# Recurrence inputs as twelve paired seven-product sums, with outputs taken partly from the PSUM banks

## The chip, the core and the metric

The kernel runs on one core of one Trainium2 chip. Its metric is device time in microseconds, from one launch to the end of its last output. It runs one layer for one sequence of 512 tokens with 1024 channels, in float32.

## What is computed

The layer is a feed-forward block, two token mixers side by side, and a second feed-forward block, each with a normalization in front and behind and a residual. Cut to what matters here:

```
h = h + 0.5 * norm(swiglu(norm(h)))                      # FFN 1, d_ff 2816
u = norm(h);  q, k, v, xr, yr, gl = split(u @ w_in)      # one wide product
attn_d = attention(q, k, v) @ w_attn_branch              # 12 heads, three dilations
xc  = causal_conv4(xr);  ga, gx = sigmoid(xc @ w_a), sigmoid(xc @ w_x)   # per head
rec = scan(a(ga), b(ga, gx, xc)) * gelu(yr);  rec_d = rec @ w_rec_branch
g0, g1 = sigmoid(gl)                                     # a gate for each branch
h = h + norm((g0 * attn_d + g1 * rec_d) @ w_out)
h = h + 0.5 * norm(swiglu(norm(h)))                      # FFN 2
```

The change concerns the columns of `w_in` that give `xr`, `yr` and the second half of `gl`: 8 + 8 + 8 column blocks of 128, each a product of a 1024 x 128 weight with the 1024 x 512 activation `u`.

## The kernel before, in words

**Numbers in two halves.** A float32 operand is split into a high part (rounded to float32r by ScalarE, L261) and a low part (VectorE subtracts, L262). A product then takes three matmuls for each block of 128 contraction rows: high x high, high x low, low x high (`mm3`, L275 to L278). `split` is one ScalarE copy and one VectorE subtract, for weights as for activations.

**Weights** come in one stream in the order of `stream_plan` (L65), in loads of 1 MB into the two buffers of tile `raw`, issued by SyncE (L207). `fetch` (L219) splits a block into tile `w8`, which has four buffers of 2 x 1024 columns (or `w4`, two of 2 x 512).

**Two kinds of product.** The plain one, `gemm` (L291), makes one block of 128 output columns with 8 x 3 matmuls of 512 columns. The other, `seven` (L594), makes a pair of output blocks, called `g` and `u`, at once: by a Strassen-like scheme with seven products p1 to p7 on halves of the channels and halves of the tokens, each 4 x 3 matmuls of 256 columns. It needs sums of the activation's quarters (made once, `forms_of`, L507) and, for each pair, sums of the weight's quarters, each split again (`w_forms`, L557, and `w_forms_in_place`, L576). A pair's weights so take three splits of 1024 columns, one of 512, and four additions of 512 on VectorE; a plain block takes one split of 1024. Before the change the FFNs use such products (in `prod`, L841, with their own code), as do the twelve pairs of q and k and the four pairs of the first gate half (L1220). The recurrence uses plain products.

**The order around the change.** After FFN 1 (to about 356 us) come the values, then for each of four heads the q and k pairs and attention, then the four gate pairs, then the product with `w_attn_branch` (eight plain products of 4 x 3 matmuls). Then the recurrence: `conv(0)`; for each head `branch`, `conv` of the next head, `gates_of`, `recur`, and the plain products of the second gate half by the table `GATE1` (L41). `conv` makes two blocks of `xr`, copies them from the bank into an order by phase (L1281), and applies four taps (L1283, L1285); `branch` makes two blocks of `yr` and copies them (L1297); `gates_of` takes 24 matmuls and four sigmoids (L1314); `recur` is a chain of ScalarE functions (L1325 to L1340), VectorE products (L1330 to L1343), a scan (L1344), and a split into `rec` (L1346). Last, the product with `w_rec_branch` (L1364), `w_out`, and FFN 2.

A scheduler orders the instructions of each engine from the written order and from priorities (`tc.high_priority`); each engine then runs its own list in that order, waiting on semaphores. Eight PSUM banks are shared: `acc_ps` (L264) hands out banks 0 to 4 in turn, `aux_ps` banks 5 to 7.

Of the kernel before, what the change touches and what calls it, by code (L numbers as in the profile page):

```python
# [40 lines left out]
GATE1 = ((), (0, 1), (2, 3), (4, 5, 6, 7))  # L41
# [7 lines left out]
def ffn_order(n):  # L49
# [4 lines left out]
    for f in range(n0, NF):  # L54
# [6 lines left out]
        order.append(("finish", f))  # L61
    return order


def stream_plan():  # L65
# [37 lines left out]
    for h in range(-1, NH):  # L103
        if h >= 0:
            for c in (2 * h, 2 * h + 1):
                plan.append((("in", 44 + c), 1024))
        if h + 1 < NH:
            for c in (2 * h + 2, 2 * h + 3):
                plan.append((("in", 36 + c), 1024))
        if h < 0:  # L110
            continue
        plan.append((("lru", h), 1024))
        for c in GATE1[h]:
            plan.append((("in", 60 + c), 1024))
# [32 lines left out]
def hybrid_layer(ctx: ExitStack, tc: tile.TileContext, xT: bass.AP, xN: bass.AP, wst: bass.AP,  # L147
# [11 lines left out]
    turns = {"acc": 0, "aux": 0}  # L159
# [104 lines left out]
    def acc_ps():  # L264
        turns["acc"] += 1
        return banks[(turns["acc"] - 1) % 5]
# [150 lines left out]
    class Boundary:  # L417
# [3 lines left out]
        def __init__(self, f, grow, his, los, kept):  # L421
            self.f, self.grow, self.his, self.los, self.kept = f, grow, his, los, kept
            self.u = {}
# [13 lines left out]
        def turn(self, b):  # L437
            for i, u in enumerate(self.u.pop(b)):
# [4 lines left out]
                hi, lo = (t[:, :, b * P:(b + 1) * P] for t in (self.his[i], self.los[i]))  # L443
# [63 lines left out]
    def forms_of(x, his, los, pool, copied):  # L507
# [8 lines left out]
        def slot():  # L516
            return tx_slot(pool, 1 if copied else 2).rearrange("p s k t -> p s (k t)").rearrange(
                "p s (b c) -> p s b c", b=2)
# [3 lines left out]
        for name, i, j in (("p1", 0, 0), ("p2", 1, 0), ("p3", 1, 1)):  # L522
            t[name] = tuple(z[i][:, :, HALVES[j]] for z in (his, los))
# [20 lines left out]
        def middle():  # L544
            form("p6", slot(), d[2])
# [48 lines left out]
    def seven(t, w, z, g, u, seen=lambda ap: ap):  # L594


        b, y = acc_ps()[:, :HB], acc_ps()[:, :HB]
# [17 lines left out]
        def sum_of(dst, ps, c):  # L615
            with tc.high_priority(offset=EVAC):
                DVE.tensor_add(dst, seen(ps), seen(c))
# [895 lines left out]
```

## Time and profile before

| | before |
|---|---|
| median of 3 runs | 1247.98 us (1246.37 to 1248.45) |
| the profiled execution's own time | 1246.12 us |
| its span, first to last instruction | 1244.4 us |
| PE busy in the span | 1221.5 us, 98% |
| VectorE (DVE) busy | 958.9 us, 77% |
| ScalarE (ACT) busy | 730.1 us, 59% |
| granted TensorE clock | 0.997 |

In the profile, PE is TensorE, PEld its weight loads, DVE is VectorE, ACT ScalarE, POOL GpSimd and SP SyncE. A row of a timeline gives the start in us, the duration, engine, line, operation, output and inputs, and in brackets how long the engine sat idle ahead of it and what ended that. Matmuls are pipelined, so their durations overlap; the time from one start to the next tells what each takes of the stream.

### The profile page before, as it was taken

What the parts mean: (1) busy time and instruction counts of PE and PEld (TensorE: products, weight loads), DVE (VectorE), ACT (ScalarE), POOL (GpSimd) and SP (SyncE); (2) the same over time, 40 slices, a digit from 0 to 9 for tenths busy, and PEclk for the clock granted to TensorE, in tenths of its full rate; (3) what the DMA queues carried; (4) which work ended last, traced back from release to release, by engine and by line L of the source; (5) the groups of instructions that cost most, each with busy time, mean ns of one, the idle gap of its engine ahead of it and who ended that gap; (6) DMA issues with size and microseconds to landing.
All of it is one profiled execution on the core that took longest, in us unless ns stands there. A gap on an engine that the chain in (4) does not pass through costs nothing.

```text
span 1244.4 us, 19101 instructions
## 1 busy us (share of the span) xinstructions
PE 1221.5 (98%) x7616; PEld 1100.5 (88%) x7616; DVE 958.9 (77%) x1510; ACT 730.1 (59%) x1215; POOL 75.6 (6%) x123
## 2 busy tenths in 40 slices
PE   9979999999999999999999999999999999999997
PEld 8878999999877899999988787888899999999996
DVE  7997798988577487898665878655788887979865
ACT  7556665664455455665545988733566565656442
POOL 0001101010102000000000000000110110101000
PEclk9999999999999999999999999999999999999999
DMA  6245646464724132222242222323462555555441
GB/s 242 102 124 148 170 122 170 135 166 123 239 114 161 68 111 78 97 81 81 91 169 102 102 102 68 104 100 143 145 220 87 151 160 150 160 141 158 114 153 67
DMA packets 35449, 162.35 MB, mean 130 GB/s; under 512 B 3872, under 2 KB 7072, under 8 KB 23328
## 3 DMA queue, kind: packets, MB, share of 16 engines
q1 hardware_dynamic: 17712, 106.08, 24.1%
q0 software_dynamic: 17648, 55.06, 16.8%
q8 instruction: 59, 0.97, 0.3%
q14 instruction: 30, 0.25, 0.1%
HBM read 150.64 MB, written 6.29 MB: 126 GB/s over the span
## 4 chain that ended last, share of the span: by engine, by line
PE 78%; DVE 10%; ACT 7%; DMA 2%; issue 2%; SPq 0%; DVEq 0%; ACTq 0%
PE bank L853 9%; PE bank L854 9%; PE bank L855 9%; PE bank L276 5%; PE bank L277 5%; PE bank L278 5%; PE bank L605 4%; PE bank L606 4%; PE bank L607 4%; PE bank L769 4%; PE bank L770 4%; PE bank L771 4%; DVE w L262 2%; DMA raw<-in_w 2%; ACT w L261 1%
## 5 line engine op out<-in xcount | busy, mean ns | idle before, releaser
L262 DVE TENSOR_TENSOR w<-raw,w 128x1024 fp32r<-128x1024 f32 (+1 forms) x275 | 297.6, 1092 | 91.5 <-ACT w L261 87.7
L261 ACT ACTIVATE w<-raw 128x1024 fp32r<-128x1024 f32 (+1 forms) x275 | 255.5, 950 | 121.9 <-PE bank L278 44.9
L853 PE MATMUL bank<-big,w 128*128 128x256 f32 x840 | 241.4, 287 | 7.1 <-DVE ub L866 3.0
L854 PE MATMUL bank<-big,w 128*128 128x256 f32 x840 | 238.1, 283 | 0.0
L855 PE MATMUL bank<-big,w 128*128 128x256 f32 x840 | 236.8, 283 | 0.0
L853 PEld LDWEIGHTS bank<-big,w 128*128 128x128 f32 x840 | 161.3, 192 | 12.5 <-DVE ub L866 5.4
L854 PEld LDWEIGHTS bank<-big,w 128*128 128x128 f32 x840 | 161.5, 192 | 1.5
L855 PEld LDWEIGHTS bank<-big,w 128*128 128x128 f32 x840 | 160.9, 192 | 0.0
L605 PE MATMUL bank<-big,w 128*128 128x256 f32 x320 | 91.9, 287 | 0.0
L606 PE MATMUL bank<-big,w 128*128 128x256 f32 x320 | 91.7, 287 | 0.0
L607 PE MATMUL bank<-big,w 128*128 128x256 f32 x320 | 90.8, 284 | 0.0
L769 PE MATMUL bank<-wd,act 128*128 128x512 f32 x224 | 87.8, 392 | 0.0
L770 PE MATMUL bank<-wd,act 128*128 128x512 f32 x224 | 87.7, 392 | 0.0
L771 PE MATMUL bank<-wd,act 128*128 128x512 f32 x224 | 87.2, 389 | 0.0
L276 PE MATMUL bank<-big,w 128*128 128x512 f32 x192 | 74.7, 389 | 0.0
L278 PE MATMUL bank<-big,w 128*128 128x512 f32 x192 | 74.7, 389 | 0.0
L277 PE MATMUL bank<-big,w 128*128 128x512 f32 x192 | 74.7, 389 | 0.0
L861 ACT ACTIVATE c<-bank 128x256 f32<-128x256 f32 x72 | 27.5, 382 | 62.4 <-PE bank L855 61.9
L605 PEld LDWEIGHTS bank<-big,w 128*128 128x128 f32 x320 | 61.2, 191 | 1.1
L606 PEld LDWEIGHTS bank<-big,w 128*128 128x128 f32 x320 | 61.3, 191 | 0.0
L607 PEld LDWEIGHTS bank<-big,w 128*128 128x128 f32 x320 | 61.3, 191 | 0.0
L262 DVE TENSOR_TENSOR wd<-npair,wd 128x1024 fp32r<-128x1024 f32 x24 | 29.4, 1223 | 39.4 <-ACT wd L261 39.4
(344 smaller groups left out, 2976.1 us busy)
## 6 DMA issues: line engine op xcount, KB each, us to landing
raw<-in_w SPq DMA_DIRECT2D x94, 1024.0 KB, 5.0
dr<-in_wdn POOLq DMA_DIRECT2D x40, 512.0 KB, 5.4
npair<-in_wdn POOLq DMA_DIRECT2D x32, 512.0 KB, 5.5
big<-act POOLq DMA_DIRECT2D x6, 512.0 KB, 3.5
h<-in_x SPq DMA_DIRECT2D x8, 256.0 KB, 5.2
h<-in_xn POOLq DMA_DIRECT2D x4, 512.0 KB, 5.2
kept_m<-h POOLq DMA_DIRECT2D x4, 512.0 KB, 2.9
h<-kept_m POOLq DMA_DIRECT2D x4, 512.0 KB, 4.3
```

The costliest lines, as they stand in the source:

```text
L261: ACT.activation(dh, src, AF.Copy)
L262: DVE.tensor_sub(dl, src, dh.bitcast(F32))
L276: PE.matmul(ps, wh, xh, start=first, stop=False)
L605: PE.matmul(ps, wh, xh, start=start and k == 0, stop=False, skip_group_check=True)
L606: PE.matmul(ps, wh, xl, start=False, stop=False, skip_group_check=True)
L607: PE.matmul(ps, wl, xh, start=False, stop=k == 3, skip_group_check=True)
L769: PE.matmul(ps, xh, wh, start=start and k == 0, stop=False, skip_group_check=True)
L770: PE.matmul(ps, xh, wl, start=False, stop=False, skip_group_check=True)
L771: i = PE.matmul(ps, xl, wh, start=False, stop=k == 1, skip_group_check=True)
L853: PE.matmul(ps, wh, xh, start=start and k == 0, stop=False, skip_group_check=True)
L854: PE.matmul(ps, wh, xl, start=False, stop=False, skip_group_check=True)
L855: i = PE.matmul(ps, wl, xh, start=False, stop=k == 3, skip_group_check=True)
```

## The change

The 24 plain products of the recurrence's stage become twelve calls of `seven`. The table `GATE1` now lists pairs, placed one behind head 1, one behind head 2, two behind head 3. `seven` itself is rewritten for all its users: the order is p1, p5, p6, p2, p7, p3, p4; two banks of four are taken in turn, and a fifth, bank 4, is held for the half that takes p1 + p2, with p1 copied into it by ScalarE (from the second pair on); two of the four outputs are read straight from a bank by ScalarE, the other two are VectorE additions of a bank and a copy. The activation's forms must outlive attention, so p6 gets a buffer of its own (`six`) and p4 one of the six large ones; the residual `h` is therefore reloaded behind the recurrence and not ahead of the product with `w_attn_branch`. The 25 small VectorE operations on `a_param` now write into `npair`, a tile that is free from the end of FFN 1.

```diff
-GATE1 = ((), (0, 1), (2, 3), (4, 5, 6, 7))
+GATE1 = ((), (0,), (1,), (2, 3))
+def rec_order():
+    def pair(c):
+        return ("pair", c, c + 1)
+    order = [pair(36)]
+    for h in range(NH):
+        order.append(pair(44 + 2 * h))
+        if h + 1 < NH:
+            order.append(pair(36 + 2 * h + 2))
+        order.append(("lru", h))
+        order += [pair(60 + 2 * g) for g in GATE1[h]]
+    return order
...
-        return banks[(turns["acc"] - 1) % 5]
+        return banks[(turns["acc"] - 1) % turns["of"]]
...
-            form("p6", slot(), d[2])
+            form("p6", slot() if copied else six, d[2])
...
-            form("p4", big([P, 2, 2, T]) if copied else slot(), d[2])
+            form("p4", big([P, 2, 2, T]), d[2])
...
-    def seven(t, w, z, g, u, seen=lambda ap: ap):
-        b, y = acc_ps()[:, :HB], acc_ps()[:, :HB]
+    def seven(t, w, y, fresh, g0, g1, u0, u1):
+        b, z, y = acc_ps()[:, :HB], acc_ps()[:, :HB], y[:, :HB]
...
         product("p1", b, True)
-        c1 = copy(b)
-        product("p2", y, True)
-        sum_of(g[0], y, c1)
+        if fresh:
+            c1 = copy(b)
+        else:
+            out(lambda: ACT.activation(y, b, AF.Copy))
+        product("p5", z, True)
+        c5 = copy(z)
         product("p6", b, False)
         c6 = copy(b)
-        product("p5", z, True)
-        c5 = copy(z)
+        product("p2", y, fresh)
...
+            out(g0, y)
         product("p7", b, False)
-        c7 = copy(b)
-        sum_of(u[1], c7, c5)
-        product("p4", y, True)
-        sum_of(u[0], y, c7)
+        out(u1, b, c5)
         product("p3", z, False)
-        sum_of(g[1], z, c6)
+        out(g1, z, c6)
+        product("p4", b, False)
+        out(u0, b)
...
-        new_h()
-        for b in range(4):
-            nc.gpsimd.dma_start(hb(b), kept_m[b])
...
         def s8(name):
-            return lpool.tile([P, 8], F32, name=name)
+            i = 8 * next(s8s)
+            return npair[:, 0, i:i + 8]
...
+        def take(ev):
+            i = events.index(ev)
+            if i + 1 < len(events):
+                request(events[i + 1])
+            return ready.pop(ev)
+        def run(key, *outs):
+            seven(t, take(key), banks[4], False, *outs)
         def conv(hd):
-            for c in (2 * hd, 2 * hd + 1):
-                ps = acc_ps()
-                gemm(ps, fetch(("in", 36 + c)), um)
...
+            run(("pair", 36 + 2 * hd, 37 + 2 * hd),
+                lambda ps: ACT.activation(g0, seen(ps), AF.Copy),
+                lambda ps, c: DVE.tensor_add(g1, seen(ps), seen(c)),
...
         lpool_cm.__exit__(None, None, None)
+        turns["of"] = 5
+        new_h()
+        for b in range(4):
+            nc.gpsimd.dma_start(hb(b), kept_m[b])
```

`request` calls `w_forms_in_place` for a pair, so while one pair is multiplied the forms of the next are made. `branch` and the gate loop are rewritten in the same way as `conv`; the second gate half's outputs go through `gate_pair`, whose straight halves ScalarE's sigmoid reads from the bank, and whose other halves VectorE adds first.

**How rows move on VectorE, in the recurrence.** These rows of before stand in VectorE's list between the recurrence of head 1 and the taps of head 3's `xr`. A subtract into `w8` (L262) is one plain block's low half; L1285 is a tap, L1297 the copy of a `yr` block, L1345 the last product of `recur`:

```order
L1297 COPY ge_6953<-bank0_73 128x512
L262 TENSOR_TENSOR rec_6336<-ge_6688,rec_6336 128x512
L1345 TENSOR_TENSOR ge_6719<-th_6831,ge_6719 128x512
L262 TENSOR_TENSOR w8_7022<-raw_6984,w8_7022 128x1024
L262 TENSOR_TENSOR w8_7060<-raw_7058,w8_7060 128x1024
L262 TENSOR_TENSOR rec_6336<-ge_6719,rec_6336 128x512
L1297 COPY ge_6982<-bank1_74 128x512
L262 TENSOR_TENSOR w8_7131<-raw_7058,w8_7131 128x1024
L262 TENSOR_TENSOR w8_7161<-raw_7159,w8_7161 128x1024
L1285 SCALAR_TENSOR_TENSOR sig_6337<-xr_7013,first_83,sig_6337 128x512 x3
```

Of the change, the rows around the taps of head 1's `xr`. Line numbers are those of the changed kernel: L267 is the subtract of a split, L1359 a tap, L589 to L593 the four additions of a pair's weight quarters (`raw_6696` holds the pair of `yr` for head 1, `raw_6784` the pair of `xr` for head 2):

```order
L267 TENSOR_TENSOR w4_6701<-raw_6696,w4_6701 128x512
L1359 SCALAR_TENSOR_TENSOR sig_6307<-xr_6582,first_83,sig_6307 128x512
L589 TENSOR_TENSOR raw_6696<-raw_6696 128x512
L1359 SCALAR_TENSOR_TENSOR sig_6307<-xr_6584,first_83,sig_6307 128x512
L590 TENSOR_TENSOR raw_6696<-raw_6696 128x512
L267 TENSOR_TENSOR w4_6789<-raw_6784,w4_6789 128x512
L592 TENSOR_TENSOR raw_6696<-raw_6696 128x512
L589 TENSOR_TENSOR raw_6784<-raw_6784 128x512
L267 TENSOR_TENSOR w8_6700<-raw_6696,w8_6700 128x1024
L593 TENSOR_TENSOR raw_6696<-raw_6696 128x512
L590 TENSOR_TENSOR raw_6784<-raw_6784 128x512
L267 TENSOR_TENSOR rec_6306<-sig_6307,rec_6306 128x512
```

Where before one subtract of 1024 columns stood for each block, there is now a run of additions and subtracts for each pair, and the taps stand between them.

**How rows move on VectorE, at the end of FFN 1.** Before, between the second product's last additions into `facc` and the last output column's sums (`u`, L866, is the sum that must have read its bank before p4 may go on in it), there stood:

```order
L786 TENSOR_TENSOR facc<-facc,bank_76 128x512
L262 TENSOR_TENSOR act<-u,act 128x512
L786 TENSOR_TENSOR facc<-facc,bank_77 128x512
L262 TENSOR_TENSOR wd_98<-raw,wd_98 128x1024
L262 TENSOR_TENSOR w_3103<-raw,w_3103 128x1024
L866 TENSOR_TENSOR u<-bank_74,c 128x256
```

In the change all the small operations on `a_param` stand ahead of the last two of these (L878 is the same sum as L866); here are the last of them and what follows:

```order
L1316 TENSOR_TENSOR npair<-npair 128x8
L1318 SCALAR_TENSOR_TENSOR npair<-npair 128x8
L1319 TENSOR_SCALAR npair<-npair 128x8
L1320 TENSOR_SCALAR npair<-npair 128x8
L267 TENSOR_TENSOR w_3103<-raw,w_3103 128x1024
L878 TENSOR_TENSOR u<-bank_74,c 128x256
```

Before, they stood behind the last gate pair, some 300 us later. On ScalarE their one Exp moves with them, with a load of its function table, to just ahead of the copy of p1 for FFN 1's last output column.

More of the change, by code (lines that the diff above doesn't have):

```diff
@@ L102, in stream_plan @@
         plan.append((("attn", m), 512))
[L103 to L114, printed above, removed]
+    for ev in rec_order():
+        plan.append((ev, 1024 if ev[0] == "lru" else 2048))
     for m in range(KC):
@@ L1081, in pair_of, with pair @@
             return forms.pop(key)
+        def pair(key, *outs):
+            seven(t, pair_of(key), banks[4], first_pair.pop() if first_pair else False, *outs)
         def qk(hd):
@@ L1289, in branch @@
         def branch(hd):
-            gel = []
-            for c in (2 * hd, 2 * hd + 1):
-                ps = acc_ps()
-                gemm(ps, fetch(("in", 44 + c)), um)
-                ge = lpool.tile([P, T], F32, name="ge", tag="ge", bufs=4)
-                with tc.high_priority(offset=EVAC):
-                    DVE.tensor_copy(ge, ps)
-                gel.append(ge)
+            gel = [lpool.tile([P, T], F32, name="ge", tag="ge", bufs=4) for _ in range(2)]
+            (g0, g1), (u0, u1) = ([x[:, h] for h in HALVES] for x in gel)
+            run(("pair", 44 + 2 * hd, 45 + 2 * hd),
+                lambda ps: ACT.activation(g0, ps, AF.Copy),
+                lambda ps, c: DVE.tensor_add(g1, ps, c),
+                lambda ps: ACT.activation(u0, ps, AF.Copy, scale=-1.0),
+                lambda ps, c: DVE.scalar_tensor_tensor(u1, ps, -1.0, c, op0=ALU.mult, op1=ALU.subtract))
             return gel
         def gates_of(hd):
-            wh, wl = fetch(("lru", hd))
+            wh, wl = take(("lru", hd))
             a_ = wh.rearrange("p (w i c) -> p w i c", w=2, i=2)
@@ L1354, in hybrid_layer @@
             recur(hd, gel, gas, gxs)
[L1355 to L1358 removed]
+            for g in GATE1[hd]:
+                gate_pair(("pair", 60 + 2 * g, 61 + 2 * g), sig, 2 * g, run)
         lpool_cm.__exit__(None, None, None)
+        turns["of"] = 5
+        new_h()
+        for b in range(4):
+            nc.gpsimd.dma_start(hb(b), kept_m[b])
         mg = act_big("mg")
```

113 lines of the change are left out of this document (74 added, 39 removed).

## The prediction, made before the changed kernel ran

> **What bounds the kernel now.** I read the page's first two parts, then the windows of the recurrence's stage, then rows of its timelines.
>
> ```profile
> PE 1221.5 (98%) x7616; PEld 1100.5 (88%) x7616; DVE 958.9 (77%) x1510; ACT 730.1 (59%) x1215; POOL 75.6 (6%) x123
> PE   9979999999999999999999999999999999999997
> DVE  7997798988577487898665878655788887979865
> ```
>
> TensorE is busy in nearly every slice, so for most of the span only matmuls taken away or added count. VectorE is the second engine. In slices 20 to 25 (622 to 809 us) it falls to 5 to 8 tenths: the attention branch's product and the recurrence.
>
> ```profile
> core 0: us, PE busy (x) PEld busy (x) DVE busy (x) ACT busy (x) POOL busy (x), PEclk, DMA share, GB/s
> 648.50:664.00 15.50, 15.50 (x70) 12.82 (x69) 9.25 (x12) 7.80 (x9) 0.00 (x0) 1.00 0.34 132
> 664.00:704.00 40.00, 39.24 (x173) 32.15 (x172) 26.31 (x38) 30.15 (x39) 0.00 (x0) 1.00 0.30 105
> 704.00:744.00 40.00, 38.44 (x170) 31.49 (x169) 33.33 (x43) 32.24 (x42) 0.00 (x0) 1.00 0.26 90
> 744.00:784.00 40.00, 39.02 (x171) 31.69 (x170) 28.70 (x36) 34.90 (x45) 0.00 (x0) 1.00 0.27 96
> 784.00:805.30 21.30, 21.30 (x95) 17.64 (x95) 17.43 (x22) 17.37 (x23) 0.00 (x0) 1.00 0.28 97
> sum 156.80, PE 153.50 PEld 125.79 DVE 115.01 ACT 122.46 POOL 0.00; mean PE 30.70 PEld 25.16 DVE 23.00 ACT 24.49 POOL 0.00
> ```
>
> This is the stage that the change rewrites, 156.8 us long. TensorE works 153.5 of it and waits some 3.3; VectorE has 115.0 and ScalarE 122.5 (columns 1, 3 and 4 of the busy times). So the stage is TensorE's, with 42 us of room on VectorE and 34 on ScalarE. What the change takes from TensorE it pays for out of that room.
>
> **What TensorE saves.** Starts of successive matmuls, first of a plain product, then of a seven-product pair, and the first matmul of the product with `w_rec_branch`:
>
> ```profile
> 648.30 0.39 PE L276 MATMUL bank<-big,w 128*128 128x512 f32 x1
> 648.53 0.39 PE L277 MATMUL bank<-big,w 128*128 128x512 f32 x1
> 604.72 0.28 PE L605 MATMUL bank<-big,w 128*128 128x256 f32 x1
> 604.84 0.28 PE L606 MATMUL bank<-big,w 128*128 128x256 f32 x1
> 805.14 0.39 PE L276 MATMUL bank<-rec,w 128*128 128x512 f32 x1
> ```
>
> A matmul of 512 columns takes 0.227 us of the stream, one of 256 takes 0.120: more than half. Two plain blocks are 48 x 0.227 = 10.9 us; a pair is 84 x 0.120 = 10.1 us. The scheme that saves an eighth of the arithmetic saves 0.8 us a pair, 12 x 0.8 = 9.6 us in all. TensorE's work in the stage becomes 12 x 10.1 + 96 x 0.227 (the gates) = 142.8 us. The Trainium skill ("TensorE: Matmul & The Clock Gate", section Back-to-back issue gap) speaks against even this: it gives about 81 ns for a sustained matmul of 128 columns and 131 for one of 512, so an estimate half-way between is some 98 ns for 256, and twelve pairs would cost 12 x (84 x 0.098 - 48 x 0.131) = 23 us more than the plain blocks, where the rows say 9.6 less. The rows have these very tiles and decide.
>
> **What VectorE pays.** Rows from the recurrence and from an FFN:
>
> ```profile
> 706.84 1.22 DVE L262 TENSOR_TENSOR w<-raw,w 128x1024 fp32r<-128x1024 f32 x1
> 707.98 1.29 DVE L262 TENSOR_TENSOR rec<-ge,rec 128x512 fp32r<-128x512 f32 x2
> 709.18 0.75 DVE L1285 SCALAR_TENSOR_TENSOR sig<-xr,first,sig 128x512 f32<-128x512 f32 x1
> 162.34 0.69 DVE L584 TENSOR_TENSOR raw<-raw 128x512 f32<-128x512 f32 x1
> 163.06 0.69 DVE L585 TENSOR_TENSOR raw<-raw 128x512 f32<-128x512 f32 x1
> 169.24 0.42 DVE L866 TENSOR_TENSOR ub<-bank,c 128x256 f32<-128x256 f32 x1
> 169.58 1.22 DVE L262 TENSOR_TENSOR w<-raw,w 128x1024 fp32r<-128x1024 f32 x1
> ```
>
> and the groups of the stage, each shape apart:
>
> ```profile
> L262 DVE TENSOR_TENSOR w<-raw,w 128x1024 fp32r<-128x1024 f32 x29 | 35.1, 1220 | 18.0 <-ACT w L261 18.0
> L261 ACT ACTIVATE w<-raw 128x1024 fp32r<-128x1024 f32 x29 | 30.5, 1058 | 8.3 <-DMA raw<-in_w 5.3 <-PE bank L278 2.5 <-ACT ge L1340 0.6
> L1281 ACT ACTIVATE xr<-bank 128x512 f32<-128x512 f32 x8 | 8.7, 1089 | 11.1 <-PE bank L278 11.1
> L1297 DVE COPY ge<-bank 128x512 f32<-128x512 f32 x8 | 5.5, 682 | 5.2 <-PE bank L278 5.2
> ```
>
> Start to start, a subtract of 1024 columns takes 1.14 us, one of 512 takes 0.60, an addition of 256 0.34; an addition of 512 columns takes 0.72 behind another one of its chain (162.34 to 163.06) and, if it stands between strangers, no less than the 0.60 of the subtract; I take 0.66. The forms of a pair cost 3 x 1.14 + 0.60 + 4 x 0.66 = 6.7 us of VectorE, two plain blocks 2.3. Of the 29 subtracts in the stage four are for the gates and two for the next product, so 23 belong to plain blocks. VectorE's sum is then: 115.0, less 23 x 1.14 = 26.2, less eight copies of `yr` at 0.60 = 4.8, plus 12 x 6.7 = 80, less 3 for the first pair's forms that are made beside the attention branch's product, plus 24 additions of 256 at 0.36 = 8.6. That is 169.6 us. ScalarE: 122.5, less 23 x 1.05 and 8.7 and some 5 for reads of whole banks, plus 12 x (3 x 1.05 + 0.63) = 45 and some 68 reads of 256 columns at 0.27, is about 148 us. Its pace for 256 columns:
>
> ```profile
> 601.22 0.37 ACT L612 ACTIVATE c<-bank 128x256 f32<-128x256 f32 x1
> 601.48 1.06 ACT L261 ACTIVATE w<-raw 128x1024 fp32r<-128x1024 f32 x1
> ```
>
> So **the bound changes hands**: 142.8 us for TensorE, 148 for ScalarE, 169.6 for VectorE. The order shown above confirms where this falls: the taps and the recurrence's products stand between the rows of the forms, and TensorE's p5 and p6 wait for those. What is not for pairs is 169.6 - 77 - 8.6 = 84 us, 21 a head. Behind head 1, with three pairs of 6.7 + 0.7 us, VectorE so owes 43 us; TensorE has 3 x 10.1 + 24 x 0.227 = 35.7.
>
> **How long the stage gets.** When VectorE is the bound it does not work all the time. The one stretch of before where it bounds, the start of FFN 1, tells how much is lost:
>
> ```profile
> 28.00:78.00 50.00, 46.58 (x242) 39.96 (x240) 47.94 (x65) 27.10 (x36) 2.60 (x4) 0.97 0.34 116
> ```
>
> It works 47.94 of 50 us, 96%. 169.6 / 0.96 = 176.9 us to the last split into `rec`. The first block of the next product needs that split only for its last eighth, 4.8 us after its start, so TensorE may begin at about 172. In the first 60 us VectorE and TensorE are nearly even and wait for each other in turn; I add 1.5, a choice. 173.6 against 156.8 is **+16.8 us**. Without any loss on VectorE it would be 169.6 - 4.8 = 164.8, or +8.0: the lower end.
>
> **The end of FFN 1.** The small operations on `a_param` cost nothing before, since they stood beside the attention branch's product. Now they stand ahead of a sum for which TensorE waits:
>
> ```profile
> 634.69 0.17 DVE L1260 TENSOR_SCALAR po<-po 128x8 f32<-128x8 f32 x1
> 634.89 0.17 DVE L1261 TENSOR_TENSOR po<-po,zz 128x8 f32<-128x8 f32 x1
> 626.35 1.28 ACT L1252 ACT_TABLE_LOAD   x1
> 314.72 1.22 DVE L262 TENSOR_TENSOR wd<-raw,wd 128x1024 fp32r<-128x1024 f32 x1 [1.50 <-ACT wd L261]
> 319.37 1.23 DVE L262 TENSOR_TENSOR w<-raw,w 128x1024 fp32r<-128x1024 f32 x1 [3.43 <-ACT w L261]
> 320.52 0.42 DVE L866 TENSOR_TENSOR u<-bank,c 128x256 f32<-128x256 f32 x1
> 320.99 0.39 PE L853 MATMUL bank<-big,w 128*128 128x256 f32 x1
> ```
>
> VectorE's split at 314.72 ends at 315.9; ScalarE's table load and Exp put off the next step to about 316.1. 26 operations at 0.20 end at 321.3; the split that stood at 319.37 ends at 322.5, the sum of 320.52 at 322.9. TensorE's p4 began at 320.99, right behind that sum, so it comes **1.8 us** late, and what follows is a full TensorE. At least 0 (if the scheduler's gaps fit better on the chip), at most 5.2, the whole row of operations.
>
> **Attention and the rest.** Its pairs keep their number of matmuls, and TensorE has no gap there:
>
> ```profile
> 480.00:520.00 40.00, 40.00 (x330) 39.35 (x329) 33.85 (x69) 23.13 (x54) 0.00 (x0) 1.00 0.24 86
> L853 PE MATMUL bank<-big,w 128*128 128x256 f32 x840 | 241.4, 287 | 7.1 <-DVE ub L866 3.0 <-DVE g L866 2.5 <-ACT c L861 0.9
> ```
>
> Fewer VectorE sums can therefore gain nothing. The new order makes p4 wait until u1 has read bank b, with p3's 1.4 us as cover, as the FFNs' products already do; those show 7.1 us of idle time in 30 pairs, 5.5 of it two single waits. The other 1.6 over 30 pairs is 0.05 a pair; the whole is 0.24. For 16 pairs that is 0.9 to 3.8 us; I take **1**. The later reload of `h` is four loads on POOL's queue:
>
> ```profile
> h<-kept_m POOLq DMA_DIRECT2D x4, 512.0 KB, 4.3
> ```
>
> The product with `w_rec_branch` (192 x 0.227 = 43.5 us) lies between them and their first use: nothing, and at the worst one landing of 4.3 us. SyncE's queue has two more loads for the same bytes, at 0.26 to 0.34 of the DMA engines' time (last but one column of the windows): nothing, unless a buffer `raw` comes free late, which is part of the ring below.
>
> **The sum.** 1246.1 + 16.8 + 1.8 + 1.0 = 1265.7 us for an execution like the profiled one. That one lies 1.9 under the median of the runs, so I give **1267**.
>
> **Rivals.** *TensorE stays the bound.* If the forms were always ready, the stage would give back 9.6 us: 1246.1 - 9.6 + 2.8 for the other two terms, 1241 with the offset. For it: the FFNs run the same forms with TensorE full. Against it: there VectorE has room, here 169.6 us do not fit into 143. It decides if VectorE needs less than 10.1 us a pair with all else, and it needs about 14. 6%. *The gain and the loss cancel*, because the subtracts and sums overlap better than start to start and ScalarE takes the strain: within some 8 us above before, 1248 to 1256. 10%. *The ring of buffers takes over.* The third `w8` of a pair takes the place of the one that p3 of the pair before has read. From the end of p3 the chain is ScalarE's copy (1.06), VectorE's subtract (1.22), p5, p2, the additions and the last split, p6, p7, p3: about 10.2 us even if both engines were free. Whatever of VectorE's other 7 us a pair falls into it adds in full: at worst 17 us a pair, 12 x 17 = 204 us less the overlap of the gates, some 195, +38: 1289. For it: VectorE runs its list in order, and taps stand inside the forms. Against it: the order puts two pairs' forms beside each other, so the chain has other work to hide in. 16%. The forecast itself, VectorE's sum with a few per cent of loss, has 68%.
>
> **Range and chances.** The forecast's own range is 1256 to 1278. To hold 8 in 10 I go from 1253, the upper part of the cancelling case, to 1284, most of the way to the ring. A measurement of this kernel can tell about 0.2%, 2.5 us, from no change. Faster: 6%, the first rival. Same: 4%, the lower part of the second. Slower: 90%.
>
> **What would show it.** In the profile after, the stage from the attention branch's product to the product with `w_rec_branch` should be about 173 us, with VectorE busy for 160 to 170 of it and TensorE for some 143, and TensorE's waits there should name VectorE's splits `w` (L267). At the end of FFN 1 there should be one wait of TensorE of 1 to 2 us for the sum `u`. I am wrong if VectorE is busy below 90% of the stage while TensorE waits (then it is the ring or ScalarE), if TensorE is full there (then the forms were cheaper than their rows), or if attention shows waits of more than 4 us.

## The result, and the profile after

The changed kernel takes 1263.71 us (median of 4 runs, 1262.35 to 1265.16) against 1247.17 us before (4 runs): a ratio of 1.0134, with a 95% interval of 1.0122 to 1.0147. It is 16.5 us slower. The prediction was 1267 with a range of 1253 to 1284. The profiled execution of the changed kernel took 1263.51 us, with a span of 1261.7 us.

From the page of the changed kernel, busy times and slices:

```profile
PE 1225.2 (97%) x8048; PEld 1120.9 (89%) x8048; DVE 1003.0 (79%) x1567; ACT 760.4 (60%) x1307; POOL 75.7 (6%) x123
PE   9979999999999999999999889899999999999997
DVE  7997798988776587788478999965688888979865
```

TensorE's row now has slices of 8 tenths in the recurrence, 22, 23 and 25 (from 694 us on), and VectorE's slices 20 to 25 show 7 to 9 in place of 5 to 8. The windows of the recurrence's stage, which begins at 650.17 us behind the attention branch's product and ends at 822.78 us with the first matmul of the product with `w_rec_branch`:

```profile
core 0: us, PE busy (x) PEld busy (x) DVE busy (x) ACT busy (x) POOL busy (x), PEclk, DMA share, GB/s
650.20:664.00 13.80, 13.28 (x105) 12.63 (x104) 13.60 (x18) 9.92 (x15) 0.00 (x0) 1.00 0.30 89
664.00:704.00 40.00, 38.55 (x290) 36.59 (x289) 35.07 (x53) 32.59 (x52) 0.00 (x0) 1.00 0.24 82
704.00:744.00 40.00, 34.67 (x241) 31.86 (x240) 39.41 (x60) 35.61 (x55) 0.00 (x0) 0.96 0.25 88
744.00:784.00 40.00, 35.43 (x241) 32.14 (x241) 36.65 (x51) 32.98 (x51) 0.00 (x0) 0.96 0.25 84
784.00:822.80 38.80, 34.16 (x237) 31.42 (x235) 36.02 (x51) 36.61 (x59) 3.60 (x6) 0.96 0.46 157
sum 172.60, PE 156.09 PEld 144.65 DVE 160.75 ACT 147.72 POOL 3.60; mean PE 31.22 PEld 28.93 DVE 32.15 ACT 29.54 POOL 0.72
```

The stage takes 172.6 us where it took 156.8. VectorE is busy for 160.8 of it (93%), ScalarE for 147.7. TensorE is held back from 704 us on. The longest of its waits in the stage (total us, times, longest):

```profile
PE bank L610 <- ACT w L266: 3.9, 9, 0.8
PE bank L610 <- ACT bank L628: 3.5, 5, 1.7
PE bank L612 <- DVE w L267: 2.5, 2, 1.3
PE bank L610 <- ACT sig L1268: 2.2, 1, 2.2
PE bank L610 <- DVE u L1263: 1.3, 1, 1.3
PE bank L610 <- DVE xr L1354: 1.1, 1, 1.1
```

Most of these name ScalarE: its copies into `w` (L266), its copy of p1 into bank 4 (L628), a sigmoid (L1268). Only 2.5 us name VectorE's splits, which the forecast expected there; another 2.4 us name VectorE's additions of a bank. With VectorE at 93% that was the first sign that the number might be right for a reason only half right. The chain of waits shows how one becomes the other; two pieces of it (start, duration, work):

```profile
714.01 1.03 DVE ge L1418
715.05 0.91 DVE w L267
...
716.11 1.27 DVE rec L267 x2
...
717.92 0.67 DVE w L267
718.60 1.20 DVE raw L589 x2
719.80 1.20 DVE raw L590 x2
721.01 0.60 DVE raw L592
721.61 0.66 DVE sig L1359
722.27 1.15 DVE w L267
723.46 0.58 PE bank L612
...
765.68 0.52 ACT w L266
766.20 0.52 ACT rec L266
766.72 0.58 ACT gt L1387
767.30 0.95 ACT w L266
768.26 0.37 ACT bank L628
768.62 1.18 ACT gt L1387 x2
```

In the first piece TensorE's matmul at 723.46 waits for a subtract that stands in VectorE's list behind a head's last product (L1418), two splits into `rec`, sums for two pairs and a tap. In the second the chain runs along ScalarE's list: weight copies between sigmoids. Both engines run their lists in order, and the chain changes from one to the other.

Another 1.5 us of the difference between the two spans (17.3 us) arise before 270 us, in instructions that the change does not touch: the same FFN 1 column begins at 268.12 us before and at 269.62 us after. The other profiles below have it at 268.9 to 271.0, the one without the recurrence's pairs at 270.51, whose runs are as fast as before; so it is no part of the loss.

### The profile page after: what moved, and what is told of

Read it like the earlier page. It is cut to its first block, busy times and chain, and to the rows that moved or that the text cites. A ratio compares the mean times of both kernels' runs of the same rounds, so it can differ in the third digit from the quotient of the medians.

```text
span 1261.7 us, 20121 instructions
## 1 busy us (share of the span) xinstructions
PE 1225.2 (97%) x8048; PEld 1120.9 (89%) x8048; DVE 1003.0 (79%) x1567; ACT 760.4 (60%) x1307; POOL 75.7 (6%) x123
## 4 chain that ended last, share of the span: by engine, by line
PE 75%; DVE 14%; ACT 6%; DMA 2%; issue 2%; SPq 0%; POOL 0%; DVEq 0%; ACTq 0%; POOLq 0%
PE bank L865 8%; PE bank L866 8%; PE bank L867 8%; PE bank L610 6%; PE bank L612 6%; PE bank L611 5%; PE bank L781 4%; PE bank L782 4%; PE bank L783 4%; DVE w L267 3%; PE bank L282 3%; PE bank L283 3%; PE bank L281 3%; PE bank L389 2%; PE bank L388 2%; PE bank L387 2%
## 5 line engine op out<-in xcount | busy, mean ns | idle before, releaser
L267 DVE TENSOR_TENSOR w<-raw,w 128x1024 fp32r<-128x1024 f32 (+1 forms) x299 | 319.7, 1080 | 66.8 <-ACT w L266 65.8
L266 ACT ACTIVATE w<-raw 128x1024 fp32r<-128x1024 f32 (+1 forms) x299 | 275.1, 941 | 102.6 <-PE bank L283 48.7
L865 PE MATMUL bank<-big,w 128*128 128x256 f32 x840 | 241.9, 288 | 8.4 <-DVE ub L878 4.2
L866 PE MATMUL bank<-big,w 128*128 128x256 f32 x840 | 238.6, 284 | 0.0
L867 PE MATMUL bank<-big,w 128*128 128x256 f32 x840 | 237.3, 284 | 0.0
L610 PE MATMUL bank<-big,w 128*128 128x256 f32 x672 | 196.3, 293 | 11.2 <-ACT bank L628 3.5
L612 PE MATMUL bank<-big,w 128*128 128x256 f32 x672 | 189.2, 286 | 2.7 <-DVE w L267 2.5
L611 PE MATMUL bank<-big,w 128*128 128x256 f32 x672 | 191.3, 285 | 0.0
L865 PEld LDWEIGHTS bank<-big,w 128*128 128x128 f32 x840 | 161.8, 193 | 13.6 <-DVE ub L878 6.7
L866 PEld LDWEIGHTS bank<-big,w 128*128 128x128 f32 x840 | 162.0, 193 | 1.5
L867 PEld LDWEIGHTS bank<-big,w 128*128 128x128 f32 x840 | 161.5, 193 | 0.0
L610 PEld LDWEIGHTS bank<-big,w 128*128 128x128 f32 x672 | 129.8, 193 | 18.2 <-ACT w L266 4.6
L612 PEld LDWEIGHTS bank<-big,w 128*128 128x128 f32 x672 | 129.0, 194 | 3.3 <-DVE w L267 3.3
L611 PEld LDWEIGHTS bank<-big,w 128*128 128x128 f32 x672 | 130.3, 194 | 0.3
L267 DVE TENSOR_TENSOR wd<-npair,wd 128x1024 fp32r<-128x1024 f32 x24 | 29.3, 1222 | 39.3 <-ACT wd L266 39.3
L281 PE MATMUL bank<-act,w 128*128 128x512 f32 (+1 forms) x168 | 58.9, 356 | 0.0
L283 PE MATMUL bank<-act,w 128*128 128x512 f32 (+1 forms) x168 | 58.5, 349 | 0.0
L282 PE MATMUL bank<-act,w 128*128 128x512 f32 (+1 forms) x168 | 58.5, 349 | 0.0
```

Of the source, the lines that this page charges most:

```text
L266: ACT.activation(dh, src, AF.Copy)
L267: DVE.tensor_sub(dl, src, dh.bitcast(F32))
L281: PE.matmul(ps, wh, xh, start=first, stop=False)
L610: PE.matmul(ps, wh, xh, start=start and k == 0, stop=False, skip_group_check=True)
L611: PE.matmul(ps, wh, xl, start=False, stop=False, skip_group_check=True)
L612: PE.matmul(ps, wl, xh, start=False, stop=k == 3, skip_group_check=True)
```

## Experiments

All were compared with the kernel before on the same chip, where that took 1246.95 to 1247.53 us; a difference from the changed kernel is one of medians, taken apart from each other. "Stage" is always from the end of the attention branch's product to the first matmul with `w_rec_branch`; of each kernel its window is shown, with the columns of the table above. Theory 1 is the forecast's (VectorE's sum), theory 2 its rival, the ring of buffers, theory 3 puts ScalarE in VectorE's place; theory 4 (three lists that wait for each other) came up after the first four runs, theory 5 ahead of the run without taps and without table loads.

**More work on VectorE, and on ScalarE.** `idle` is memory that nobody reads; the second kernel has `ACT.activation(idle, xc, AF.Copy)` in the same place.

```diff
                 split(rec.hi[c], rec.lo[c], xc)
+                for _ in range(3):
+                    DVE.tensor_scalar(idle, xc, 1.0, None, op0=ALU.mult)
```

> The changed kernel with 24 more VectorE instructions in the recurrence: behind the split of each block of xr, three scaled copies of 512 columns into memory that nobody reads. Nothing waits for them, TensorE's, ScalarE's and the buffers' work is the same. At 0.35 to 0.65 us each they are 8 to 16 us of VectorE. Theory 1, VectorE's sum bounds the stage: the stage of 172.6 us grows by most of that, 0.8 to 1 of what VectorE is busy longer, and the kernel with it. Theory 2, the ring of w8 buffers bounds it: only the part that falls between a copy and its subtract counts, about a third to a half, 3 to 7 us. Theory 3, ScalarE bounds it (TensorE's waits name its copies most): 0 to 3 us.

> The changed kernel with 24 more ScalarE instructions at the same places, copies of 512 columns into memory that nobody reads: at 0.55 to 0.63 us about 13 to 15 us of ScalarE, on top of the 147.7 of 172.6 us that it is busy. Theory 1 (VectorE's sum): ScalarE stays below VectorE's 160.8 us or equals it, so the stage grows by 0 to 5 us. Theory 2 (ring): the copies that fall into the chain count, 3 to 7 us. Theory 3 (ScalarE): 12 to 15 us.

```profile
651.40:837.50 186.10, 162.49 (x1106) 150.27 (x1104) 170.43 (x255) 155.08 (x233) 3.58 (x6) 0.93 0.28 97
```

```profile
650.50:832.50 182.00, 161.99 (x1106) 150.84 (x1105) 160.49 (x229) 157.23 (x248) 3.59 (x6) 0.92 0.30 99
```

1275.73 us (ratio 1.0228, 1.0211 to 1.0245) and 1272.08 us (1.0186, 1.0163 to 1.0210): 12.0 and 8.4 us more than the changed kernel. VectorE's busy time rose by 9.7 us and the stage by 13.5; ScalarE's by 9.5 and the stage by 9.4. Theory 1 comes nearest in the first run and fails on the second, theory 3 the other way round. So work on either engine counts; how much of it is not told apart here. In the first kernel ScalarE is busier too, by 7.4 us, with 26 table loads in the stage in place of 23 (the second has 19), and in both a good part of the added time stands at a lower clock (0.93 and 0.92 in the windows), which the last section takes up.

**Less work on VectorE: no taps.**

```diff
-                for t_ in (2, 1, 0):
-                    DVE.scalar_tensor_tensor(xc, xr[:, t_:t_ + T], col("cw", t_ * 8 + c), xc,
-                                             op0=ALU.mult, op1=ALU.add)
```

> The changed kernel without the 24 taps of the convolution (its output is not the reference's): 24 x 0.745 = 17.9 us less on VectorE, none of it in the chain of a pair's forms; ScalarE, TensorE and the buffers keep their work. Theory 1 (VectorE's sum): VectorE's work in the stage falls from 160.8 to 143 us, level with TensorE and ScalarE, and the stage from 172.6 to 157 to 160 us, 12 to 16 less. Theory 2 (ring): 3 to 7 less, what stood inside the chain. Theory 3 (ScalarE): 0 to 3 less.

```profile
650.90:823.80 172.90, 153.47 (x1106) 142.88 (x1104) 147.57 (x209) 150.03 (x231) 3.58 (x6) 0.98 0.31 105
```

1265.49 us (1.0143, 1.0121 to 1.0166): nothing gained. VectorE has 13.2 us less and the stage is as long as before the edit. No engine is busy above 89%. Theory 1 falls with this run: if VectorE's sum set the stage, 12 to 16 us had to go.

**Six wide weight buffers.** `two` are two fixed tiles.

```diff
-            a, b, c, d = w8(), w8(), w8(), w4()
+            a, b, c, d = w8(), wide.pop() if wide else w8(), w8(), w4()
...
+            if ev[0] == "pair":
+                wide[:] = [two[next(third) % 2]]
```

> The changed kernel with the ring of weight buffers taken apart: the third wide tile of each recurrence pair (for p6 and p3) gets two buffers of its own, so six stand where four stood. The room comes from the activation forms of p4 and p7, in whose place p5's is read, in attention too (the output is not the reference's); the number of instructions in the stage is the same. Theory 1 (VectorE's sum): the stage stays within 0 to 3 us of 172.6. Theory 2 (ring): VectorE can work ahead, and the stage falls by 8 us or more. Theory 3 (ScalarE): 0 to 3 us.

```profile
649.50:824.50 175.00, 154.25 (x1106) 144.59 (x1104) 163.18 (x233) 155.49 (x235) 3.58 (x6) 0.96 0.31 103
```

1267.63 us (1.0162, 1.0143 to 1.0181). The stage is 2.4 us longer, not 8 shorter: the ring of buffers is not what holds TensorE, and theory 2 falls.

**Without the sums of weight quarters, without table loads, and without both.** The first does no sums (L589, L590, L592, L593) for the keys of the recurrence; the second ("no table loads") replaces functions there, for instance

```diff
-                ACT.activation(th, ga, AF.Tanh, scale=sp4[:, c:c + 1])
+                ACT.activation(th, ga, AF.Identity, scale=sp4[:, c:c + 1])
```

> The changed kernel without the four sums of weight quarters of each of the recurrence's twelve pairs (its output is not the reference's): 48 x 0.68 = 32.7 us less of the 160.8 us of VectorE in the stage, and each pair's chain of forms shorter by them; ScalarE keeps 147.7 us, TensorE its matmuls. Theory 1 (VectorE's sum): the bound goes to ScalarE or TensorE, the stage falls from 172.6 to 150 or less, 20 us or more off the kernel, which is then at the time of before. Theory 3 (ScalarE): 0 to 3 us. Theory 4, formed after the kernel without taps lost nothing: VectorE's, ScalarE's and TensorE's lists run in order and wait for each other, and the stage takes 1.15 to 1.17 times the busiest of them; ScalarE's 147.7 us then give about 170, 3 us less, and more only as far as the shorter chain helps.

> The changed kernel with all functions that need a table in the recurrence and its gates (sigmoid, tanh, exp, square root, gelu) replaced by copies that need none (its output is not the reference's): 23 loads x 1.28 = 29.5 us less of the 147.7 us of ScalarE; VectorE keeps 160.8 us. Theory 1 (VectorE's sum): the stage falls by 0 to 5 us, to the 96% of VectorE. Theory 3 (ScalarE): by 15 us or more. Theory 4 (three lists): some of the waits of VectorE's recurrence for ScalarE go, 3 to 8 us.

> The two edits together, no sums of weight quarters in the recurrence's pairs and no table loads in the recurrence (its output is not the reference's): VectorE about 128 us, ScalarE about 118 us, TensorE's matmuls 142.8 us, so only TensorE is left. Theory 1 (VectorE's sum): no more than the kernel without the sums. Theory 3 (ScalarE): no more than the kernel without table loads. Theory 4 (three lists): clearly more than either and more than the two added up: 145 to 150 us for the stage, 23 to 28 less, the kernel at 1237 to 1242 us. All three: if the stage cannot come below 143 us, TensorE's saving of 0.8 us a pair was rightly read from the rows.

```profile
650.50:816.80 166.30, 150.53 (x1106) 141.65 (x1104) 133.30 (x184) 147.49 (x229) 3.58 (x6) 0.97 0.32 110
```

```profile
649.90:818.50 168.60, 152.11 (x1106) 141.98 (x1104) 162.08 (x232) 123.19 (x208) 3.60 (x6) 0.99 0.30 107
```

```profile
650.10:801.50 151.40, 145.66 (x1107) 139.48 (x1106) 134.99 (x186) 120.68 (x207) 3.59 (x6) 1.00 0.36 122
```

1258.45 us (1.0092, 1.0077 to 1.0107), 1260.96 us (1.0119, 1.0100 to 1.0137) and 1241.44 us (0.9958, 0.9943 to 0.9972). Of the stage the first takes 6.3 us, the second 4.0, both together 21.2: twice as much as the two added up. This is what theory 4 asked for, though a little less of it (it wanted 23 to 28), and neither single-engine theory allows it; theory 3 falls with the second run, which takes 24.5 us off ScalarE. It is also the only kernel here whose recurrence in seven products is faster than plain products, and it leaves out work for that.

**Is it the engines' load, or the length of one pair's chain?** The sums stand inside the chain of a pair's forms, so the last run could mean either. Taps and table loads do not stand in it:

> The changed kernel without the 24 taps and without table loads in the recurrence (its output is not the reference's). It is the pair of reliefs that leaves a pair's chain of forms as it is: VectorE 147 us, ScalarE 123 us, TensorE's matmuls 142.8 us; alone the first gave 0 us of the stage and the second 4.0. Theory 4 (three lists, the load of both engines counts): much more than the two added up, 10 to 16 us off the stage, the kernel at 1249 to 1254 us. Theory 5, what counts is the length of a pair's chain of forms (the sums gave 6.4 us, and with the tables 21.2, since the chain was shorter): no more than the two added up, 4 to 5 us, the kernel at about 1259 to 1261 us.

```profile
650.40:807.50 157.10, 148.58 (x1106) 140.69 (x1105) 145.44 (x206) 119.71 (x203) 3.60 (x6) 1.00 0.34 114
```

1251.59 us (1.0036, 1.0022 to 1.0049): 15.5 us off the stage, where alone the two edits gave none and 4.0. Theory 5, by which the length of the chain alone counts, falls; the load of both engines counts.

**The sums on GpSimd.**

```diff
+            adder = nc.gpsimd if key[0] == "pair" else DVE
-            DVE.tensor_add(u1, u0, u1)
+            adder.tensor_add(u1, u0, u1)
```

(and the other three sums likewise)

> The changed kernel with the 48 sums of weight quarters of the recurrence's pairs on GpSimd, which is idle there, in place of VectorE; nothing is left out. No run shows a sum on GpSimd; I expect 1 to 2 us each against 0.68 on VectorE, so a pair's chain gets 1 to 5 us longer while VectorE has 32.7 us less. Theory 1 (VectorE's sum): 10 to 20 us less than the changed kernel. Theory 2 (ring, chain of a pair): slower than the changed kernel by up to 12 us. Theory 4 (three lists): about the same, within 6 us either way, since the shorter list and the longer chain stand against each other.

The stage, then two groups of it by line and shape, and the taps' group of the changed kernel:

```profile
649.90:859.80 209.90, 166.68 (x1106) 153.73 (x1104) 159.15 (x181) 152.98 (x231) 81.46 (x54) 0.90 0.26 86
```

```profile
L1360 DVE SCALAR_TENSOR_TENSOR sig<-xr,first,sig 128x512 f32<-128x512 f32 x24 | 29.9, 1283 | 1.1 <-ACT sig L1358 0.9
...
L593 POOL TENSOR_TENSOR raw<-raw 128x512 f32<-128x512 f32 x12 | 21.2, 1771 | 14.2 <-DVE w L267 13.5
```

```profile
L1359 DVE SCALAR_TENSOR_TENSOR sig<-xr,first,sig 128x512 f32<-128x512 f32 x24 | 17.7, 745 | 2.0 <-ACT sig L1357 1.9
```

1300.87 us (1.0432, 1.0416 to 1.0447): 37 us slower than the changed kernel, worse than any theory said. A sum takes 1.56 to 1.77 us on GpSimd, by its line, and while it runs VectorE's own instructions stretch: a tap takes 1.283 us on average where it took 0.745. So VectorE, with the 48 sums gone, is busy for 159.2 us, hardly less than the 160.8 before. That does not explain the 37 us, though: the busy times of VectorE and ScalarE together are 312.1 us, against 308.5 in the changed kernel. What else is different is a pair's chain, in which each of four sums now takes about 1 us longer and passes between two engines; that the length of this chain is the reason is likely, but no run shows it apart.

**Only the order changed.**

```diff
-        with tc.high_priority(offset=AHEAD):
+        with tc.high_priority(offset=300 if key[0] == "pair" else AHEAD):
```

> The changed kernel with nothing but the order changed: the forms of the recurrence's pairs get a priority 300 ahead in place of 100, so that on VectorE and ScalarE they stand earlier, ahead of taps and of parts of the recurrence that stood ahead of them. Same instructions, same durations. Theory 1 (VectorE's sum): within 2 us of the changed kernel. Theory 4 (three lists): TensorE waits less for forms and more for the gates and at the end of the stage; a change of 3 us or more in either direction, I think less time by 3 to 8 us.

```profile
650.00:825.80 175.80, 154.52 (x1106) 145.36 (x1105) 161.37 (x231) 148.65 (x228) 3.57 (x6) 0.94 0.30 103
```

and of its waits the longest:

```profile
PE bank L281 <- ACT w L266: 10.0, 1, 10.0
```

1266.24 us (1.0153, 1.0139 to 1.0167). With the same work the stage is 3.2 us longer, and TensorE now waits once for 10.0 us, for the gates' weights, where the longest wait of the changed kernel was 2.2. So the order moves the waits, as theory 4 has it, though it went the other way than I expected, and 3.2 us is little more than the 2 us that theory 1 allows. It also gives a measure of caution: each edit above lets the scheduler order the lists anew (the kernel with more work on VectorE also has 26 table loads in its stage where the changed kernel has 23), so a single difference of 3 us in the stage decides nothing. The gaps between 10.3 and 21.2 us above, and between 4.0 and 15.5, are well beyond that.

**The other parts alone, and three pairs alone.** In both the small operations stand behind the last gate pair again:

```diff
-            return npair[:, 0, i:i + 8]
+            if i >= 48:
+                return lpool.tile([P, 8], F32, name=name)
+            return sig[:, KC - 1, i:i + 8]
```

> The other parts alone: attention's pairs in the new form, the residual reloaded late, but the recurrence's twelve pairs as 24 plain products of 512 columns, as before; and the small operations on a_param back behind the last gate pair (in a slice of a tile that is free there). Room in memory comes from five tiles in place of six for the gates. If the recurrence's pairs are the whole loss: the time of before, 1246 to 1249 us, within 0.2%, its stage at 156 to 158 us, and attention as long as in the changed kernel, within 0.3 us. If attention's new form costs 1 us or more, as its lower bound in the prediction had it: 0.1 to 0.3% above before. At the end of FFN 1 the wait of TensorE for the sum u (0.52 us, p4 later by 1.35 us) should be gone.

> The kernel of the other parts alone, and of the recurrence's pairs only the first three (xr of head 0, yr of head 0, xr of head 1) in seven products, where before VectorE was busy for 9.3 of 15.5 and 26.3 of 40 us and ScalarE for 7.8 and 30.2. TensorE has 3 x 0.8 = 2.4 us less, VectorE some 14 us more. Theory 4 (three lists): with TensorE at 150, VectorE at 130 and ScalarE at 128 us TensorE stays well ahead of both, and most of the saving is kept: 1 to 2.4 us below the kernel of the other parts alone, 0.1 to 0.2%, at the edge of what can be told; this may be faster than both kernels. If already three pairs make TensorE wait, it is equal or slower by up to 3 us.

```profile
651.00:808.50 157.50, 153.56 (x674) 125.79 (x673) 117.88 (x178) 121.94 (x156) 1.42 (x2) 1.00 0.27 95
```

```profile
651.20:811.60 160.40, 153.99 (x781) 130.50 (x780) 129.28 (x199) 130.37 (x174) 3.58 (x6) 0.99 0.31 113
```

1247.11 us (ratio 1.0001, 0.9992 to 1.0010) and 1247.73 us (1.0006, 0.9997 to 1.0015). The first says that the recurrence's pairs are the whole loss; its attention takes 221.9 us, as in the changed kernel. The second says that even three of them, placed where both engines had the most room, save nothing that can be told, where theory 4 had expected 1 to 2.4 us: by the medians that kernel is 0.6 us slower than the first. In the profile the three pairs take 32.0 us of TensorE (651.19 to 683.21) where six plain blocks took 32.6 (650.94 to 683.58), not 30.2, and the rest of the stage is longer by more than that; but the profiled execution took 1251.15 us, the longest of 11, so the size of that last part is not certain. No mixture is shown to beat the kernel before.

## Why the prediction was right, step by step

**The stage: the size was right (+15.8, forecast +16.8), the reason only in part.** Right were the counts: VectorE busy for 160.8 us (forecast 160 to 170), ScalarE for 147.7 (148), TensorE no longer full (though busy for 156.1 us, not the 143 of the forecast). The step that failed is "How long the stage gets": the stage was taken as VectorE's sum over its 96%, with ScalarE 21 us away from mattering. That the size came out is partly luck, since two misses offset each other. Up to the last split into `rec` (828.95 us) VectorE is busy for 166.4 us, where the forecast had 169.6, and it stands idle for 7% of that time, where the forecast had 4%: 178.8 us in place of 176.9. The runs put both engines in the place of the one:

| kernel | VectorE busy | ScalarE busy | both | stage | stage / both |
|---|---|---|---|---|---|
| more on VectorE | 170.4 | 155.1 | 325.5 | 186.1 | 0.57 |
| more on ScalarE | 160.5 | 157.2 | 317.7 | 182.0 | 0.57 |
| six wide buffers | 163.2 | 155.5 | 318.7 | 175.0 | 0.55 |
| only the order | 161.4 | 148.7 | 310.0 | 175.8 | 0.57 |
| the changed kernel | 160.8 | 147.7 | 308.5 | 172.6 | 0.56 |
| no taps | 147.6 | 150.0 | 297.6 | 172.9 | 0.58 |
| no table loads | 162.1 | 123.2 | 285.3 | 168.6 | 0.59 |
| no sums | 133.3 | 147.5 | 280.8 | 166.3 | 0.59 |
| no taps, no table loads | 145.4 | 119.7 | 265.1 | 157.1 | 0.59 |
| no sums, no table loads | 135.0 | 120.7 | 255.7 | 151.4 | 0.59 |

In these kernels the stage is 0.55 to 0.59 of the two busy times together, whichever of the two the work is on, while against VectorE alone it runs from 1.04 (no table loads) to 1.25 (no sums). The forecast's 96% came from FFN 1, where ScalarE has 27 of 50 us, and so does not tell what happens where both have above 85%. Theory 4's own number, a factor on the busiest engine, was loose as well: 1.04 to 1.15. The ratio is no law either: the kernel with the sums on GpSimd stands at 0.67 and the one with three pairs at 0.62, and without sums and table loads TensorE itself, with 142.8 us of matmuls in 151.4, is close to setting the stage.

The lower clock is a rival for the gain of both reliefs, since in the kernels with two reliefs it does not fall at all. The starts of TensorE's matmuls settle it. At 0.120 us for each of the 1008 of 256 columns and 0.227 for each of the 96 of 512 they are 142.8 us. Beyond that, matmuls start late for two reasons that can be told apart: TensorE sat idle ahead of them for more than 0.15 us, or the clock was at half. In us, over the stage:

| kernel | late behind waits | late at half clock |
|---|---|---|
| the changed kernel | 20.0 | 4.5 |
| no sums | 18.0 | 1.8 |
| no table loads | 19.8 | 1.8 |
| no sums, no table loads | 6.9 | 0 |
| no taps | 22.0 | 2.9 |
| no taps, no table loads | 10.2 | 0 |

Of the waits the single reliefs take 2.0 and 0.1 us, both together 13.0; without taps the waits grow by 2.0, without taps and table loads they fall by 9.8. So the gain of both is one of waits, and the clock only adds to it. With more work on VectorE the waits have 27.1 and the half clock 10.9 us, with more on ScalarE 23.6 and 11.4.

That the chain passes from one list to the other is shown in the two pieces above; that this is why the sum counts is argued, not shown.

**TensorE's saving of 9.6 us did not arrive.** It was read rightly from the starts of matmuls, but it needs forms that are always ready. With VectorE and ScalarE both relieved the stage is 5.4 us shorter than before, the most that was seen of it. In the changed kernel the 142.8 us become 172.6 by 20.0 us behind waits, 4.5 at half clock (below) and 5.3 in shorter delays. One word beside it is wrong in the prediction: its 98 ns for 256 columns is in proportion to the columns, not half-way between its two figures; half-way is 106 ns, which makes 31 us in place of 23 and changes nothing else.

**The end of FFN 1: +1.8 forecast, 0.3 measured.** The rows there:

```profile
322.16 0.17 DVE L1320 TENSOR_SCALAR npair<-npair 128x8 f32<-128x8 f32 x1
...
323.36 0.42 DVE L878 TENSOR_TENSOR u<-bank,c 128x256 f32<-128x256 f32 x1
...
323.83 0.39 PE L865 MATMUL bank<-big,w 128*128 128x256 f32 x1 [0.52 <-DVE u L878]
```

(Of the small operations on `a_param` 30 stand on VectorE, 26 of them behind the Exp; the 25 named ahead of the prediction is too few. By the prediction's own steps the sum ends at 322.9, 1.9 us behind 320.99, not 1.8.) The mechanism is there: the last small operation, the split, the sum `u`, and TensorE behind it. But TensorE waits 0.52 us, not 1 to 2: p4 begins 2.84 us later than before, of which 1.5 had arisen by 270 us and 0.7 are three matmuls of FFN 1's last product that now stand ahead. From the column that begins at 268.12 or 269.62 to the first attention pair (426.50 or 428.27) it is 158.38 us before and 158.65 after. In the kernel of the other parts alone, where the small operations stand behind the last gate pair, the wait is gone, p4 begins 52.9 us behind that column as before (54.2 in the changed kernel), and from there to the first attention pair it is 158.57 us. The kernels that have the operations ahead take 158.27 to 158.67, so what they cost on this way cannot be told from nothing. The forecast left out that TensorE's own list changes there too and fills part of the time with other work.

**Attention: +1.0 forecast, 0.1 measured.** From its first pair to the end of the branch's product it takes 221.80 us before and 221.90 after. The lower bound of 0.05 us a pair, 0.9 us for 16, was no bound: p3 covers the read of bank b, all but 0.1 us in the whole of attention.

**The reload of `h`: nothing, as forecast.** From the end of the product with `w_rec_branch` to the end of the span it is 395.7 us before and 394.5 after; the 1.2 us less are not explained.

**Not forecast: 0.9 us in the product with `w_rec_branch`,** 44.4 us in place of 43.5. It starts slowly and waits 0.5 us for the last split into `rec`, at its last eighth, where the forecast had put that split's need.

**The rivals.** The ring was wrong (six buffers do not shorten the stage). That TensorE stays the bound, and that gain and loss cancel, are out by the result.

## What to carry to other kernels

Where two engines feed a third through in-order lists and both are busy above 85%, do not forecast from the busier one alone: relieve each in an experiment, then both, because the gain of both can be twice the sum of the single ones, as it was here. A scheme that saves an eighth of the matmuls pays only while the engines that prepare its operands have room; here plain products with 115 and 122 us of preparation in 157 ran TensorE full, and 161 and 148 us did not; 129 and 130 us, with three pairs, saved nothing that could be told. An idle GpSimd is no free adder beside a busy VectorE.

## What the hardware showed that was not expected

**Short waits halve TensorE's clock for the next microseconds.** Rows of TensorE in the changed kernel:

```profile
744.41 0.28 PE L611 MATMUL bank<-big,w 128*128 128x256 f32 x1
744.53 0.28 PE L612 MATMUL bank<-big,w 128*128 128x256 f32 x1
747.02 0.39 PE L610 MATMUL bank<-big,w 128*128 128x256 f32 x1 [2.21 <-ACT sig L1268]
...
747.36 0.41 PE L612 MATMUL bank<-big,w 128*128 128x256 f32 x1
747.56 0.41 PE L610 MATMUL bank<-big,w 128*128 128x256 f32 x1
...
751.00 0.28 PE L611 MATMUL bank<-big,w 128*128 128x256 f32 x1
751.12 0.28 PE L612 MATMUL bank<-big,w 128*128 128x256 f32 x1
```

Ahead of the wait of 2.21 us a matmul of 256 columns starts every 0.12 us, behind it every 0.21 us, until about 750.9; then 0.12 again. Windows there show the granted clock (third column from the end) at half:

```profile
743.90:747.30 3.40, 1.19 (x10) 0.99 (x9) 3.40 (x6) 3.34 (x7) 0.00 (x0) 1.00 0.00 0
747.40:750.70 3.30, 2.84 (x14) 2.55 (x13) 3.30 (x5) 2.48 (x4) 0.00 (x0) 0.50 0.00 0
```

The stage of the changed kernel has three such stretches of 3.41 us, from 723.5, 747.4 and 802.0 us; with both engines relieved it has none. So late forms cost their wait and can cost a slow stretch behind it. The Trainium skill ("TensorE: Matmul & The Clock Gate", section What's actually happening) says that the clock falls after at least one idle window of about 3.4 us. The length of the stretches agrees, but no window had to be idle here: no single wait of the stage was longer than 2.21 us, and in the 3.4 us ahead of the three stretches TensorE was busy for 1.72, 1.19 and 1.72 us. The traces of all fourteen kernels tell the same between 600 and 900 us, cut into windows of 3.41 us in step with the clock's changes. Of 1192 windows at full clock, all 29 in which TensorE was busy below 47% stand ahead of a window at half clock, and none of the 1154 above 51.5% does.

**GpSimd's sums stretch VectorE's instructions,** a tap from 0.745 to 1.283 us, as the experiment above shows. The timeline tells them apart: the 16 taps that a sum on GpSimd overlaps take 1.55 us on average (13 of them 1.65 to 1.79, three 0.74 to 0.75), the other 8 take 0.74. The Trainium skill ("GPSIMD Engine Reference", section Key points) says that the two share their memory interfaces and contend where a VectorE instruction has two inputs in SBUF (the on-chip memory of the tiles). The trace agrees: a tap has two, while the four additions there that read one input from a PSUM bank under a running sum take their usual 0.41 to 0.42 and 0.61 us.
